# Spacing of the weight and activation buffers in SBUF: 8,192 to 8,288 bytes and 4,096 to 4,128 bytes

## The chip, the core and the metric

The kernel runs on one core of a Trainium2 chip. The metric is the device time of one execution in microseconds (us), median of three runs. TensorE multiplies (a weight load and a matmul are two instructions), VectorE (DVE), ScalarE (ACT) and GpSimd (POOL) do the elementwise work, and SyncE (SP) issues the loads from HBM into SBUF, the on-chip memory of 128 partitions. All byte addresses below are addresses within one partition.

## The reference

A two-layer decoder trunk on 256 tokens and 1,024 channels, all in float32. Each layer has a half-step SwiGLU block, a mixer (a gated linear recurrence in layer 0, causal pooling in layer 1), a second SwiGLU block, and a gated per-layer input:

```
for i in range(DEPTH):                                   # DEPTH = 2, D = 1024, D_FF = 2816, D_RNN = 1280
    h = h + 0.5 * swiglu(rms_norm(h, ffn1_norm[i]), ffn1_w_gate[i], ffn1_w_up[i], ffn1_w_down[i])
    hn = rms_norm(h, mix_norm[i])
    m = rglru_mixer(hn, ...) if i % 2 == 0 else pool_mixer(hn, ...)
    h = h + m
    h = h + 0.5 * swiglu(rms_norm(h, ffn2_norm[i]), ffn2_w_gate[i], ffn2_w_up[i], ffn2_w_down[i])
    gate = sigmoid(rms_norm(h, ple_norm[i]) @ ple_w_gate[i])
    h = h + gate * (p[i] @ ple_w_proj[i])
return rms_norm(h, final_norm)
```

## The kernel before

The activations lie transposed, channels on the partitions and the 256 tokens along the free axis. The weights come as units of 128 x 1,024 float32 (512 KB) in the order in which they are used. A unit is loaded into one of five buffers `raw` (`load`), and `split` makes of it two float32r halves, `hl[:, 0]` = the rounded value (ACT, line 272) and `hl[:, 1]` = the rest (DVE, line 273), in one of six buffers `hl`. The normalised input of a projection is split in the same way by `put` (ACT line 320, DVE line 321) into one of seven buffers `x`: high and low half, two column blocks of 256 tokens each. One product of a weight block with an activation block is then three matmuls in `mm3`: high x high, high x low, low x high. All of them are issued by the helper line 294. In each, a 128 x 128 block of `hl` is the stationary operand, 512 contiguous bytes a partition, loaded by a LDWEIGHTS of its own, and 256 columns of `x` (in the gate, up, recurrence and PLE projections), of `hid` (the down projection of the SwiGLU blocks), of `yr` and `ytp` (the recurrence's output projection) or of another `hl` unit (`pp`, the per-layer input) are the moving operand, 1,024 contiguous bytes. In `v` of the pooling mixer the sides are exchanged. Two kinds of matmul differ: `ri`, the gates of the recurrence, has plain float32 operands (`raw` and `xc`) and takes two passes, and `po`, the pooling operator, moves 144, 128 or 16 columns of an `hl` unit against a stationary `vhl`.

The order of the weights is written out in `stream_order`; loads run seven units ahead of use and splits four. The tile framework places a pool's buffers one behind the other, each rounded up to a multiple of 32 bytes. The kernel pads its narrow tiles to a multiple of 128 bytes itself:

```
LINE = 32
...
def lines(n):
    return -(-n // LINE) * LINE
```

In the program as it is built before the change, the six `hl` start at byte 40,064 + 8,192 i, the seven `x` at 101,504 + 4,096 j, and `hid`, `yr` and `ytp` behind them; each of these is 128 modulo 512, as the five `raw` are. A block of `hl` starts at a multiple of 512 bytes in its buffer and a block of a moving tile at a multiple of 1,024, so the distance from the stationary to the moving operand of these matmuls is 0 modulo 512. Two tiles lie elsewhere: the four `vhl` at 256 modulo 512, and the extra `raw` buffers of the recurrence's gates at 384.

Of the kernel before, what the change touches and what calls it, by code (L numbers as in the profile page):

```python
# [10 lines left out]
F32R = mybir.dt.float32r  # L11
# [4 lines left out]
P = 128  # L16
D = 1024
S = 256
# [10 lines left out]
U = 1024  # L29
# [92 lines left out]
def width(key):  # L122
    if key[0] == "lru_gates":
        return min(8, len(GATE_BLOCKS[key[1]]) - 8 * key[2]) * P
    if key[0] == "ple_in":
        return 2 * S
    if key[0] == "pool_op":
        return 4 * (POOL_COLS[key[1]][1] - POOL_COLS[key[1]][0])
    return U
# [81 lines left out]
def trunk(ctx: ExitStack, tc: tile.TileContext, xT, vec, w, out):  # L211
# [4 lines left out]
    hlp = ctx.enter_context(tc.tile_pool(name="hl", bufs=6))  # L216
    hp = ctx.enter_context(tc.tile_pool(name="h", bufs=6))
    xp = ctx.enter_context(tc.tile_pool(name="x", bufs=7))
# [27 lines left out]
    def vcol(name, i):  # L246
        c = VCOL[name] + i
        return vt[:, c:c + 1]
# [15 lines left out]
    def split(n, parts=1):  # L264
        if n not in raws:
            return
        raw = raws.pop(n)
        hl = hlp.tile([P, 2, U], F32R, tag="hl", name=f"hl{n}")
        step = width(ORDER[n]) // parts
        for i in range(parts):  # L270
            c = slice(i * step, (i + 1) * step)
            nc.scalar.activation(hl[:, 0, c], raw[:, c], AF.Copy)  # L272
            nc.vector.tensor_tensor(hl[:, 1, c], raw[:, c], hl[:, 0, c].bitcast(F32), op=ALU.subtract)  # L273
        units[ORDER[n]] = hl

    def unit(*key):
        n = state["used"]
        assert ORDER[n] == key, (ORDER[n], key)
        for what, do, ahead in (("loaded", load, LOADS_AHEAD), ("split", split, SPLITS_AHEAD)):
            while state[what] < min(n + ahead + 1, len(ORDER)):  # L280
                do(state[what])
                state[what] += 1
        state["used"] = n + 1
        return units.pop(key)
# [22 lines left out]
    class Norm:  # L307
# [6 lines left out]
            self.late = None  # L314

        def put(self, j, h, square=True):
            xt = xp.tile([P, 2, 2, S], F32R, tag="x", name=f"x{self.sid}_{j}")
            for c in range(2):
                g = vcol(self.name, 2 * j + c)
                nc.scalar.activation(xt[:, 0, c], h[:, c], AF.Copy, scale=g)  # L320
                nc.vector.scalar_tensor_tensor(  # L321
                    xt[:, 1, c], h[:, c], g, xt[:, 0, c].bitcast(F32), op0=ALU.mult, op1=ALU.subtract)
            self.x[j] = xt
            if square:
                self.square(j, h)
# [505 lines left out]
    load_x(0)  # L831
    load(0, 2)
    split(0, 4)
    load_x(1)
    load(1, 2)
    split(1, 4)
    load(2)
    load(3)
# [39 lines left out]
```

## Time and profile before

| | before |
|---|---|
| median of three runs | 982.45 us (982.06 to 984.19) |
| the profiled execution, its own time | 983.27 us |
| span from its first to its last instruction | 981.5 us |
| TensorE matmul / weight load busy | 967.3 us / 960.1 us |
| DVE / ACT / POOL busy | 652.4 us / 491.5 us / 54.8 us |
| mean granted TensorE clock | 0.996 |

The profiled execution's own time is 1.8 us longer than its span and 0.8 us above the median of the three runs. Matmuls overlap in the pipeline, so the busy share of TensorE says little; the time from one start to the next is what counts. A row that merges n instructions of a kind gives their first start and, in the chain of work, the time that n of them took.

### The profile page before, as it was taken

What the parts mean: (1) busy time and instruction counts of PE and PEld (TensorE: products, weight loads), DVE (VectorE), ACT (ScalarE), POOL (GpSimd) and SP (SyncE); (2) the same over time, 40 slices, a digit from 0 to 9 for tenths busy, and PEclk for the clock granted to TensorE, in tenths of its full rate; (3) what the DMA queues carried; (4) which work ended last, traced back from release to release, by engine and by line L of the source; (5) the groups of instructions that cost most, each with busy time, mean ns of one, the idle gap of its engine ahead of it and who ended that gap; (6) DMA issues with size and microseconds to landing.
All of it is one profiled execution on the core that took longest, in us unless ns stands there. A gap on an engine that the chain in (4) does not pass through costs nothing.

```text
span 981.5 us, 18712 instructions
## 1 busy us (share of the span) xinstructions
PE 967.3 (99%) x7888; PEld 960.1 (98%) x7888; DVE 652.4 (66%) x853; ACT 491.5 (50%) x634; POOL 54.8 (6%) x48
## 2 busy tenths in 40 slices
PE   9999999999999999999999999999989999999997
PEld 9999999999999999999998999999989999999996
DVE  6956555597887655655579756555578755555585
ACT  7544444468785444543456444444448544434443
POOL 1000000023201000000021000000011000000020
PEclk9999999999999999999999999999999999999999
DMA  8866556554435655565535655565524765655511
GB/s 294 281 210 190 179 179 189 167 178 172 151 114 168 204 192 172 193 197 189 175 126 173 215 178 188 173 193 172 183 90 146 242 192 171 195 190 174 192 44 44
DMA packets 49188, 173.63 MB, mean 177 GB/s; under 512 B 5584, under 2 KB 6224, under 8 KB 49104
## 3 DMA queue, kind: packets, MB, share of 16 engines
q1 hardware_dynamic: 48960, 172.29, 54.1%
q8 instruction: 61, 1.00, 0.4%
q14 instruction: 23, 0.19, 0.1%
q10 hardware_dynamic: 144, 0.15, 0.1%
HBM read 171.37 MB, written 1.05 MB: 176 GB/s over the span
## 4 chain that ended last, share of the span: by engine, by line
PE 72%; issue 20%; DVE 6%; ACT 1%; DMA 1%; POOL 0%; SPq 0%; DVEq 0%; ACTq 0%; POOLq 0%
PE up0ffn L294 13%; PE gate0ffn L294 13%; PE acc0ffn L294 12%; PE up1ffn L294 6%; PE gate1ffn L294 6%; PE acc1ffn L294 6%; PE accl L294 3%; PE gb L294 2%; PE ri L294 2%; DVE x L321 2%; PE x L294 2%; DVE hl L273 2%; PE pp L294 1%; PE xb L294 1%; PE ple L294 1%
## 5 line engine op out<-in xcount | busy, mean ns | idle before, releaser
L273 DVE TENSOR_TENSOR hl<-raw,hl 128x1024 fp32r<-128x1024 f32 (+1 forms) x326 | 385.6, 1200 | 242.0 <-ACT hl L272 242.0
L272 ACT ACTIVATE hl<-raw 128x1024 fp32r<-128x1024 f32 (+1 forms) x326 | 331.9, 1035 | 413.2 <-issue 103.0
L294 PE MATMUL gate1ffn<-x,hl 128*128 128x256 f32 x1056 | 132.6, 284 | 2.2 <-DVE x L321 2.1
L294 PE MATMUL gate0ffn<-x,hl 128*128 128x256 f32 x1056 | 132.5, 284 | 0.3 <-ACT x L320 0.2
L294 PEld LDWEIGHTS gate1ffn<-x,hl 128*128 128x128 f32 x1056 | 129.0, 192 | 3.2 <-DVE x L321 3.0
L294 PE MATMUL up1ffn<-x,hl 128*128 128x256 f32 x1056 | 132.0, 283 | 0.0
L294 PE MATMUL up0ffn<-x,hl 128*128 128x256 f32 x1056 | 131.3, 283 | 0.0
L294 PE MATMUL acc0ffn<-hid,hl 128*128 128x256 f32 x1056 | 130.3, 283 | 0.0
L294 PEld LDWEIGHTS gate0ffn<-x,hl 128*128 128x128 f32 x1056 | 129.1, 192 | 1.0 <-ACT x L320 0.4
L294 PE MATMUL acc1ffn<-hid,hl 128*128 128x256 f32 x1056 | 130.0, 283 | 0.0
L294 PEld LDWEIGHTS up1ffn<-x,hl 128*128 128x128 f32 x1056 | 128.9, 192 | 0.0
L294 PEld LDWEIGHTS up0ffn<-x,hl 128*128 128x128 f32 x1056 | 128.6, 192 | 0.0
L294 PEld LDWEIGHTS acc0ffn<-hid,hl 128*128 128x128 f32 x1056 | 128.2, 192 | 0.2
L294 PEld LDWEIGHTS acc1ffn<-hid,hl 128*128 128x128 f32 x1056 | 128.2, 192 | 0.0
L334 POOL TENSOR_TENSOR sacc<-sq,sq 128x512 f32<-128x512 f32 x9 | 14.3, 1588 | 844.8 <-ACT sq L329 844.8
L321 DVE SCALAR_TENSOR_TENSOR x<-h,vt,x 128x256 fp32r<-128x256 f32 x64 | 48.7, 800 | 7.1 <-ACT x L320 7.1
L294 PE MATMUL ple<-x,hl 128*128 128x256 f32 x384 | 47.5, 284 | 0.0
L294 PEld LDWEIGHTS ple<-x,hl 128*128 128x128 f32 x384 | 46.6, 192 | 0.0
L466 ACT ACTIVATE hid<-gs 128x512 fp32r<-128x512 f32 x44 | 27.9, 634 | 16.4 <-DVE gs L464 16.3
L320 ACT ACTIVATE x<-h,vt 128x256 fp32r<-128x256 f32 x64 | 28.4, 496 | 6.0 <-DMA vt<-vec 2.5
L464 DVE TENSOR_TENSOR gs<-th,gs 128x512 f32<-128x512 f32 x44 | 30.4, 692 | 1.4
L467 DVE TENSOR_TENSOR hid<-gs,hid 128x512 fp32r<-128x512 f32 x44 | 30.1, 685 | 0.0
(132 smaller groups left out, 692.8 us busy)
## 6 DMA issues: line engine op xcount, KB each, us to landing
raw<-w SPq DMA_DIRECT2D x320, 512.0 KB, 4.2
raw<-w SPq DMA_DIRECT2D x7, 256.0 KB, 4.5
h<-xT SPq DMA_DIRECT2D x4, 256.0 KB, 6.5
out<-hg SPq DMA_DIRECT2D x3, 256.0 KB, 2.8
raw<-w SPq DMA_DIRECT2D x1, 288.0 KB, 2.6
raw<-w SPq DMA_DIRECT2D x2, 128.0 KB, 4.4
out<-hg SPq DMA_DIRECT2D x2, 128.0 KB, 2.0
vt<-vec ACTq DMA_DIRECT2D x1, 148.0 KB, 4.4
```

The costliest lines, as they stand in the source:

```text
L272: nc.scalar.activation(hl[:, 0, c], raw[:, c], AF.Copy)
L273: nc.vector.tensor_tensor(hl[:, 1, c], raw[:, c], hl[:, 0, c].bitcast(F32), op=ALU.subtract)
L294: nc.tensor.matmul(o, lhsT, rhs, start=self.first, stop=self.left == 0, skip_group_check=True)
L320: nc.scalar.activation(xt[:, 0, c], h[:, c], AF.Copy, scale=g)
L321: nc.vector.scalar_tensor_tensor(xt[:, 1, c], h[:, c], g, xt[:, 0, c].bitcast(F32), op0=ALU.mult, op1=ALU.subtract)
L334: nc.gpsimd.tensor_tensor(acc, self.acc, sq, op=ALU.add)
L464: nc.vector.tensor_tensor(gs, th, gs, op=ALU.mult)
L466: nc.scalar.activation(hid[:, 0], gs, AF.Copy)
L467: nc.vector.tensor_tensor(hid[:, 1], gs, hid[:, 0].bitcast(F32), op=ALU.subtract)
```

## The change

The tile of a weight unit is allocated 24 floats (96 bytes) longer, that of an activation 8 floats (32 bytes) longer, and the same view as before is cut out of the front. No instruction is added or removed, and each engine's instructions stand in the same order as before.

```diff
-        hl = hlp.tile([P, 2, U], F32R, tag="hl", name=f"hl{n}")
+        hl = hlp.tile([P, 2 * U + 24], F32R, tag="hl", name=f"hl{n}")[:, :2 * U].rearrange("p (v u) -> p v u", v=2)
...
-            xt = xp.tile([P, 2, 2, S], F32R, tag="x", name=f"x{self.sid}_{j}")
+            xt = xp.tile([P, 4 * S + 8], F32R, tag="x", name=f"x{self.sid}_{j}")[:, :4 * S].rearrange("p (v c s) -> p v c s", v=2, c=2)
```

In the program as it is built with the change, the start addresses modulo 512 are:

| tiles | before | changed |
|---|---|---|
| six `hl` | 128, all | 128, 224, 320, 416, 0, 96 |
| seven `x` | 128, all | 192, 224, 256, 288, 320, 352, 384 |
| `hid`, `yr`, `ytp`, `xc`, `gs`, `th`, `sq`, `hg` and the rest behind `x` | 128 | 416 |
| residual `h` (between `hl` and `x`) | 128 | 192 |
| `vhl` of the pooling mixer | 256 | 32 |
| `raw` of the recurrence's gates | 384 | 160 |
| `raw`, vectors | 128 | 128 |

## Rows read from the trace of the kernel before

**Rows 1.** The page's first lines: span, and busy time of each engine.

```profile
span 981.5 us, 18712 instructions
PE 967.3 (99%) x7888; PEld 960.1 (98%) x7888; DVE 652.4 (66%) x853; ACT 491.5 (50%) x634; POOL 54.8 (6%) x48
```

**Rows 2.** The page's slices: TensorE's granted clock in tenths, 40 equal slices.

```profile
PEclk9999999999999999999999999999999999999999
```

**Rows 3.** Groups of matmuls by shape: stationary and moving names, count, busy us, mean ns.

```profile
L294 PE MATMUL gate1ffn<-x,hl 128*128 128x256 f32 x1056 | 132.6, 284 | 2.2 <-DVE x L321 2.1
...
L294 PE MATMUL acc0ffn<-hid,hl 128*128 128x256 f32 x1056 | 130.3, 283 | 0.0
...
L294 PE MATMUL ple<-x,hl 128*128 128x256 f32 x384 | 47.5, 284 | 0.0
L294 PE MATMUL accl<-yr,hl 128*128 128x256 f32 x160 | 28.9, 283 | 0.0
L294 PE MATMUL gb<-x,hl 128*128 128x256 f32 x192 | 23.5, 284 | 0.0
...
L294 PE MATMUL accl<-ytp,hl 128*128 128x256 f32 x80 | 22.6, 283 | 0.0
L294 PE MATMUL x<-x,hl 128*128 128x256 f32 x144 | 17.9, 284 | 0.0
L294 PE MATMUL pp<-hl,hl 128*128 128x256 f32 x96 | 13.4, 303 | 0.0
```

**Rows 4.** The chain that ended last: start us, us, engine, tile, count.

```profile
43.95 5.76 PE up0ffn L294 x48
...
187.96 11.52 PE acc0ffn L294 x96
...
223.90 11.23 PE ri L294 x52
...
280.90 28.79 PE accl L294 x240
```

**Rows 5.** Timeline of the weight loads around the pooling operator: start us, us, count.

```profile
744.35 4.55 PEld L294 LDWEIGHTS po<-hl,vhl 128*128 128x128 f32 x40
748.83 0.66 PEld L294 LDWEIGHTS pp<-hl,hl 128*128 128x128 f32 x5
```

**Rows 6.** The tile po: count, shortest, median and longest duration ns, forms.

```profile
L294 PE MATMUL po<-hl,vhl x40: 216/276/308, 744.5 to 748.8; 128*128 128x144 f32 x16, 128*128 128x128 f32 x16, 128*128 128x16 f32 x8
```

**Rows 7.** Lines 680, 630 and 632: count, shortest, median and longest duration ns.

```profile
L680 ACT ACTIVATE r<-r,zero,sp_sp x10: 585/588/601, 237.7 to 275.3; 128x256 f32<-128x256 f32 x10
...
L630 ACT ACTIVATE xc<-xbs,vt x10: 582/587/601, 218.7 to 249.1; 128x256 f32<-128x256 f32 x10
...
L632 DVE SCALAR_TENSOR_TENSOR xc<-xbs,vt,xc x30: 456/479/486, 219.4 to 253.1; 128x256 f32<-128x256 f32 x30
```

**Rows 8.** Who waited for whom, TensorE: us in total, times, longest us.

```profile
PE v L294 <- DVE x L321: 2.6, 4, 0.8
PE gate1ffn L294 <- DVE x L321: 2.1, 4, 0.7
PE spread L378 <- DVE dg L377: 1.3, 1, 1.3
```

**Rows 9.** The page's costliest groups, splits of weights: busy us, mean ns.

```profile
L273 DVE TENSOR_TENSOR hl<-raw,hl 128x1024 fp32r<-128x1024 f32 (+1 forms) x326 | 385.6, 1200 | 242.0 <-ACT hl L272 242.0
L272 ACT ACTIVATE hl<-raw 128x1024 fp32r<-128x1024 f32 (+1 forms) x326 | 331.9, 1035 | 413.2 <-issue 103.0
```

**Rows 10.** The page's DMA issues: count, KB each, us from issue to landing.

```profile
raw<-w SPq DMA_DIRECT2D x320, 512.0 KB, 4.2
...
h<-xT SPq DMA_DIRECT2D x4, 256.0 KB, 6.5
out<-hg SPq DMA_DIRECT2D x3, 256.0 KB, 2.8
```

## The prediction, made before the changed kernel was run

> **What bounds the kernel now.** I read the page's first lines, then the groups of matmuls, then the chain of waits, then single stretches of the timeline. [...] The longest waits of TensorE for another engine come to 2.6, 2.1 and 1.3 us in all [rows 8]. So TensorE's own pace sets the end, and the question is what sets that pace.
>
> The chain gives it without the overlap of the pipeline: 48 matmuls of an up projection in 5.76 us, 96 of a down projection in 11.52, 240 of the recurrence's output in 28.79 [rows 4]. Each is 120 ns from start to start, to a tenth, whichever tiles feed it. The groups shown with 256 columns of a float32r operand count 6 x 1,056 (gate, up and down in both layers; two of the six rows stand there) + 384 + 160 + 192 + 80 + 144 + 96 = 7,392 matmuls [rows 3]; three small groups are left out. 7,392 x 0.120 = 887.0 us, 90% of the span. Nothing else in the kernel has such a lever: one ns on this pace is 7.4 us of the end.
>
> What is in the 120 ns? Two other rows bound its two halves. The gates of the recurrence, plain float32 in two passes, take 11.23 us for 52 [rows 4], 216 ns for one; the load of the weights hides under them, so the moving side alone needs at most 108 ns a pass, if a pass streams half of that time. And where the pooling operator moves few columns, the loads set the pace: the first of 40 starts at 744.35, the load after the last at 748.83 [rows 5], 4.48 us / 40 = 112 ns. So 120 is 8 ns more than the longer of the two halves, at a place where both operands are read at once and where their distance is 0 modulo 512. Those 8 ns are all that a better placing could win: 7,392 x 8 = 59.1 us.
>
> **The change part by part.** *Instructions and order:* none is added, removed or moved, so no wait is added and no queue is passed. Cost 0.
>
> *The distance of the two operands.* After the change the down projections read `hid` at 416 against `hl` at six different starts, the gate and up projections 42 pairs. No row of before shows 256 columns at another distance than 0, so the cost is bounded. The nearest row is the pooling operator: its `vhl` lies at 256, its moving blocks at 128 plus 64 bytes per group of channels in the first half of the tokens (576 bytes a group), so the four groups are 384, 448, 0 and 64 apart. Its matmuls move 144, 128 or 16 columns [rows 6], and its 40 loads come at 112 ns over the whole stretch [rows 5]. If distance 0 cost the third group's ten loads the 8 ns in question, or the other distances cost the other thirty as much, the mean would be 2 or 6 ns above that of the rest; but all forty come at 112 ns, without a break in the row, 8 ns below the pace of the long matmuls on either side. Distance 0 in one group of the four doesn't bring the 120 back. I choose 0 for the distance, since this row is the nearest. The bounds stay: a gain of up to 8 ns a matmul, and a loss for which there is no row with 256 columns.
>
> [...]
>
> *The starts themselves.* Before, all these operands start on the 128-byte grid that the kernel keeps for its narrow tiles. After it, four of six `hl` (224, 320, 416, 96), five of seven `x` and all of `hid`, `yr` and `ytp` start off it, at other multiples of 32. On TensorE the rows that touch this are again the pooling operator's: its second and fourth group move blocks that start 64 bytes off the grid, and the mean of its loads doesn't show it. But no row shows a *weight* block off the grid, so a loss there is open from 0 upward. On ACT two rows compare directly: line 680 reads 256 elements from the grid with a scale and a bias column, line 630 does the same from 12 bytes off it, and they take 588 and 587 ns [rows 7]. On DVE line 632 reads the same tile from 8, 4 and 0 bytes past the grid, and its 30 instructions lie between 456 and 486 ns with a median of 479 [rows 7]. An engine that needed a further access for a crossed line would show it in these. I take 0 for ACT and DVE. Cover, if it were not: the splits take 1,200 ns on DVE and 1,035 on ACT for 326 units [rows 9], four units ahead of use; 10 ns more on each of DVE's 326 would be 3.3 us out of the 329 us in which DVE isn't busy (981.5 - 652.4, [rows 1]). Uncovered are the `x` tiles at the layer boundaries: some 64 instructions of line 321, of which TensorE waited for eight; 10 ns on each of the eight is 0.1 us.
>
> *DMA.* The main `raw` buffers don't move, so the 320 loads of 512 KB [rows 10] write where they did. `h`, the extra `raw` of the gates and the output tiles move. Their loads run ahead of use, except that of `h` at the start (6.5 us to landing) and the stores at the end (2.8 us) [rows 10]; a hundredth on these is 0.1 us. I take 0.
>
> **The sum.** 0 + 0 + 0 on the profiled execution's 983.27 us (span 981.5 and 1.8 around it). That execution stands 0.8 us above the median of 982.45 us, so I forecast the median, **982.5 us**.
>
> **The rivals.** *Slower: a weight block off the grid costs its load something.* The load is the longer half (112 against 108), so what it loses, the pace loses. For: no row excludes it, and every one of the 7,392 matmuls has an operand off the grid except where one of the two aligned `hl` meets an aligned `x`. Against: ACT, DVE and the moving side of `po` show nothing. Price: the smallest step that the trace can show is 1 ns; 7,392 x 1 = 7.4 us, so **989.9 us**. It decides (0.2% is 2.0 us, about what a measurement of this kernel can tell from no change) from 2.0 / 7,392 = 0.27 ns a matmul. [...]
>
> [...]
>
> *Faster: the 8 ns are two reads at distance 0 in each other's way.* For: 120 is above both halves, and the two reads begin together in each matmul. Against: the third group of `po` has distance 0 too and its loads aren't longer. The whole price, 59.1 us, would give 923.3; but the pooling rows leave room for a part at most, and I choose a quarter, 2 ns a matmul: 14.8 us, so **967.7 us**. It decides from the same 0.27 ns.
>
> [...]
>
> *The change doesn't do what it says.* If the allocator rounded tiles up to 512 bytes, nothing would move. The starts in the changed program exclude that, so it gets no chance of its own. That the new starts don't touch the pace is the forecast itself.
>
> **How the numbers follow.** No change within 0.2%: 0.54, from the 112 ns over four distances and the equal ACT and DVE rows. Slower: 0.25, since no row shows a weight block off the grid, and a quarter of a ns decides. Faster: 0.21, since 8 ns are unexplained. The range reaches to the slower rival's 1 ns (989.9) and, on the other side, to nearly the faster rival's 2 ns (967.7): 970 to 990. Left out is somewhat over a half of the faster case and a quarter of the slower one, some 0.17 together. The likeliest case alone lies between 980.5 and 984.4.
>
> **What would show it.** In the changed trace's chain, 48 up or down matmuls in 5.76 us and 240 of the recurrence's output in 28.79 confirm the forecast. A pace that differs by `hl` buffer, with a period of six units, 5.9 us here and 5.76 there, would speak for a cost of starts or distances; a uniform change of the pace would speak for distances only if the down projections, with one `hid` start against six `hl`, differ from the gates. ACT's and DVE's splits should stay at 1,035 and 1,200 ns. The forecast is wrong if the pace moves by more than a quarter of a ns, either way; it would then be the step that carries over the pooling operator's short matmuls to 256 columns.

## The result, and the profile after

The changed kernel takes 970.42 us (969.80 to 971.52, three runs) against 982.45: a ratio of 0.9875, 95% interval 0.9852 to 0.9898. It is 12.0 us faster. The forecast was no change; the time lies in the range, at its lower end, near where the *faster* rival stood (967.7). One execution of one experiment kernel further down (the first under "Setting the pace from distance 0") took 2,393.67 us where its other three took 969.85 to 970.90; it is left out of that kernel's numbers, and as it is the one that was traced, no pace is read from that kernel.

The page's first lines of the changed kernel, and three of its costliest groups:

```profile
span 968.6 us, 18712 instructions
PE 952.8 (98%) x7888; PEld 944.8 (98%) x7888; DVE 652.1 (67%) x853; ACT 491.5 (51%) x634; POOL 55.5 (6%) x48
PEclk9999999999999999999999999999998999999999
L273 DVE TENSOR_TENSOR hl<-raw,hl 128x1024 fp32r<-128x1024 f32 (+1 forms) x326 | 385.6, 1201 | 234.6 <-ACT hl L272 234.6
L272 ACT ACTIVATE hl<-raw 128x1024 fp32r<-128x1024 f32 (+1 forms) x326 | 332.2, 1036 | 398.9 <-issue 97.2
L294 PEld LDWEIGHTS up1ffn<-x,hl 128*128 128x128 f32 x1056 | 127.3, 188 | 0.0
```

DVE and ACT are as busy as before [rows 1, 9], to a ns per split, so the off-grid starts cost them nothing, as forecast. What shrank is TensorE: matmuls from 967.3 to 952.8 us, loads from 960.1 to 944.8. A weight load is recorded with 188 ns, where the kernel before has 192:

```profile
L294 PEld LDWEIGHTS up1ffn<-x,hl 128*128 128x128 f32 x1056 | 128.9, 192 | 0.0
```

The clock doesn't explain it: the mean granted clock was 0.996 before and 0.994 in this execution.

The timeline of TensorE's matmuls in layer 0 of the changed kernel (start us, us, tile, count) shows the pace itself:

```profile
65.97 5.84 PE L294 MATMUL acc0ffn<-hid,hl 128*128 128x256 f32 x48
71.64 5.83 PE L294 MATMUL gate0ffn<-x,hl 128*128 128x256 f32 x48
77.31 5.85 PE L294 MATMUL up0ffn<-x,hl 128*128 128x256 f32 x48
83.00 5.84 PE L294 MATMUL acc0ffn<-hid,hl 128*128 128x256 f32 x48
```

Read the first column: from one down projection to the next 144 matmuls take 83.00 - 65.97 = 17.03 us, 118.3 ns each, where it was 120.0 [rows 4]. Over all 7,584 float32r matmuls with 256 columns the intervals from start to start add up to 922.5 us before and 909.8 after (a sum of the trace's starts): 12.7 us less, and the span is 12.9 shorter. So the gain lies between the starts of these matmuls. The pace alone would give more: some 7,490 of the intervals are between 110 and 130 ns long, and their mean fell by 1.98 ns, which is 14.8 us. The others, most of them longer, took 23.2 us before and 25.9 after. That is no more than two kernels at the same 120 ns further down differ in (19.0 us in the one at distance 0 off the grid, 25.2 in the one at 256), so no cause is read from it.

The prediction's sign for distances, down projections that differ from the gates, doesn't show in these rows: their starts are 5.67 to 5.69 us apart, whatever the tile. Each row of 48 mixes two `hl` buffers and up to four `x` buffers, so it mixes distances too.

The prediction's nearest row, the pooling operator, did not change. The weight loads there:

```profile
735.18 4.55 PEld L294 LDWEIGHTS po<-hl,vhl 128*128 128x128 f32 x40
739.65 0.66 PEld L294 LDWEIGHTS pp<-hl,hl 128*128 128x128 f32 x5
```

40 loads in 4.47 us, 112 ns, as in [rows 5], although `hl` and `vhl` lie elsewhere now. At no distance that they have in either kernel do the loads beside these short matmuls show what the long ones show.

Sorted by distance, the trace of the changed kernel says more. The table takes the intervals of 110 to 130 ns between two successive 256-column float32r matmuls, by the distance of the block that is being loaded (for the next matmul) from the moving operand of the matmul that is running, modulo 256 bytes, stationary minus moving start. *Settled* is the mean from the seventh interval on of stretches that stay at one distance (modulo 512) for ten or more.

| distance modulo 256 | intervals | mean ns | settled ns |
|---|---|---|---|
| 0 | 1,356 | 119.0 | 119.6 to 119.7 |
| 32 | 732 | 118.2 | 118.1 |
| 64 | 908 | 115.7 | 113.9 and 116.0 |
| 96 | 1,295 | 118.0 | 117.9 to 118.2 |
| 128 | 638 | 118.5 | 118.5 |
| 160 | 1,031 | 119.6 | 119.9 to 120.2 |
| 192 | 916 | 117.0 | 117.6 to 117.8 |
| 224 | 608 | 117.2 | 116.5 to 116.9 |

Where two numbers stand, they are the two distances modulo 512, which hardly differ, but for 64. The starts themselves matter little beside it: at distance 32 the settled means lie between 118.0 and 118.5 ns over six different pairs of starts modulo 256, and at no distance but 64 do they spread by more than 1.5 ns. This gave the theory that the experiments test: **the pace of a long matmul depends on the distance between the stationary block being loaded and the moving operand being read, with a period of 256 bytes, and 0 is among the worst**. (A matmul's own two operands are at the same distance in all but the matmuls at a change of buffer, so the runs don't tell the two readings apart.) Rivals: the starts themselves (off the 128-byte grid), the spreading as such, or the shift of the other buffers.

### The profile page after: what moved, and what is told of

Same layout as the page of the kernel before. It is cut to its first block, busy times and chain, and to the rows that moved or that the text cites. A ratio compares the mean times of both kernels' runs of the same rounds, so it can differ in the third digit from the quotient of the medians.

```text
span 968.6 us, 18712 instructions
## 1 busy us (share of the span) xinstructions
PE 952.8 (98%) x7888; PEld 944.8 (98%) x7888; DVE 652.1 (67%) x853; ACT 491.5 (51%) x634; POOL 55.5 (6%) x48
## 4 chain that ended last, share of the span: by engine, by line
PE 65%; issue 20%; DVE 9%; ACT 3%; DMA 1%; POOL 0%; SPq 0%; DVEq 0%; ACTq 0%; POOLq 0%
PE up0ffn L294 13%; PE gate0ffn L294 13%; PE acc0ffn L294 12%; PE up1ffn L294 6%; PE gate1ffn L294 6%; PE acc1ffn L294 6%; DVE hl L273 3%; DVE x L321 2%; PE x L294 2%; PE accl L294 1%; PE pp L294 1%; PE ri L294 1%; ACT hl L272 1%; PE ple L294 1%; DMA h<-xT 1%
## 5 line engine op out<-in xcount | busy, mean ns | idle before, releaser
L273 DVE TENSOR_TENSOR hl<-raw,hl 128x1024 fp32r<-128x1024 f32 (+1 forms) x326 | 385.6, 1201 | 234.6 <-ACT hl L272 234.6
L272 ACT ACTIVATE hl<-raw 128x1024 fp32r<-128x1024 f32 (+1 forms) x326 | 332.2, 1036 | 398.9 <-issue 97.2
L294 PE MATMUL gate0ffn<-x,hl 128*128 128x256 f32 x1056 | 130.5, 281 | 0.7 <-ACT hl L272 0.5
L294 PEld LDWEIGHTS gate1ffn<-x,hl 128*128 128x128 f32 x1056 | 127.0, 188 | 3.6 <-DVE x L321 3.0
L294 PEld LDWEIGHTS gate0ffn<-x,hl 128*128 128x128 f32 x1056 | 126.9, 189 | 1.5 <-ACT hl L272 0.7
L294 PE MATMUL acc0ffn<-hid,hl 128*128 128x256 f32 x1056 | 128.2, 281 | 0.0
L294 PE MATMUL acc1ffn<-hid,hl 128*128 128x256 f32 x1056 | 126.6, 279 | 0.0
L294 PEld LDWEIGHTS acc0ffn<-hid,hl 128*128 128x128 f32 x1056 | 126.0, 189 | 0.2 <-ACT hid L466 0.2
L294 PEld LDWEIGHTS acc1ffn<-hid,hl 128*128 128x128 f32 x1056 | 124.7, 189 | 0.0
```

The lines of the kernel that those rows point to most:

```text
L294: nc.tensor.matmul(o, lhsT, rhs, start=self.first, stop=self.left == 0, skip_group_check=True)
```

## The experiments

All kernels compute the whole reference; only addresses differ. Where several runs share a chip, the kernel before took 982.9 to 983.1 us there.

**Distance 64 everywhere.** The kernel before, with unused bytes between the `h` and the `x` pool:

```diff
+    ctx.enter_context(tc.tile_pool(name="gap", bufs=1)).tile([P, 112], F32, name="gap")
     xp = ctx.enter_context(tc.tile_pool(name="x", bufs=7))
```

> Kernel before with 448 unused bytes between the residual and the activation buffers: weight buffers 8,192 apart at 128 modulo 512 as before, all moving tiles at 64, so stationary minus moving start is 64 modulo 512 in nearly every matmul. Distance theory (period 256): the changed kernel's stretches at 64 modulo 256 ran at 113 to 114 ns from start to start, so 48 matmuls take 5.44 us and the time is 982.45 - 7,584 x 6.6 ns = 932 us. Theory that only spreading over many distances helps, or that weight blocks off the 128-byte grid are what is quicker: no spread here and no weight block off the grid, so 982 us (5.76 us for 48).

959.27 us (956.50 to 963.33), ratio 0.9768 (0.9731 to 0.9805). One constant distance, no spread and all weight blocks on the grid beat the changed kernel; so neither the spreading nor weight blocks off the grid are needed for the gain. (The moving tiles are off it here, at 64; the next kernel and the last two, whose moving tiles are on it, answer that.) But 932 was missed by 27 us. The timeline of the matmuls shows why:

```profile
373.85 5.82 PE L295 MATMUL up0ffn<-x,hl 128*128 128x256 f32 x48
379.50 5.82 PE L295 MATMUL acc0ffn<-hid,hl 128*128 128x256 f32 x48
385.16 5.92 PE L295 MATMUL pp<-hl,hl 128*128 128x256 f32 x48
390.92 5.63 PE L295 MATMUL gate0ffn<-x,hl 128*128 128x256 f32 x48
...
401.82 5.60 PE L295 MATMUL acc0ffn<-hid,hl 128*128 128x256 f32 x48
407.26 5.60 PE L295 MATMUL gate0ffn<-x,hl 128*128 128x256 f32 x48
412.70 5.60 PE L295 MATMUL up0ffn<-x,hl 128*128 128x256 f32 x48
```

Up to 385 the starts are 5.65 us apart, 117.7 ns a matmul; behind `pp` (two `hl` units, distance 0, 5.76 us or 120 ns) they are 5.44 apart, 113.3 ns. The same distance has two steady paces, and each holds for hundreds of matmuls until something interrupts. The changed kernel's trace had both already: of its 29 stretches of ten or more at 64, 14 settled at 113.2 to 113.4 ns and 15 at 117.6 to 117.8. The means of 113.9 and 116.0 in the table hid that, and the expectation took the fast one for all. In this execution 1,614 of 7,513 intervals were at 115 ns or less.

**Distance 0 off the grid.** The same spare tile, of 32 bytes, ahead of the weight buffers, so that all operands start at 160 modulo 512.

```diff
+    ctx.enter_context(tc.tile_pool(name="gap", bufs=1)).tile([P, 8], F32, name="gap")
     hlp = ctx.enter_context(tc.tile_pool(name="hl", bufs=6))
```

> Kernel before with 32 unused bytes ahead of the weight buffers: all weight and moving tiles start at 160 modulo 512, 32 bytes off the 128-byte grid, at distance 0 as before. Distance theory: 120 ns, 982.5 us, within 0.2%. Theory of the starts (off the grid is quicker): the gain of the changed kernel, 970 us or less. If a weight block off the grid cost something: above 984.5 us.

982.25 us, ratio 1.0002 (0.9988 to 1.0015). Starts 32 bytes off the grid neither help nor hurt; the prediction's *slower* rival falls with the theory of the starts.

```profile
95.61 5.92 PE L295 MATMUL up0ffn<-x,hl 128*128 128x256 f32 x48
101.37 5.92 PE L295 MATMUL acc0ffn<-hid,hl 128*128 128x256 f32 x48
107.13 5.92 PE L295 MATMUL gate0ffn<-x,hl 128*128 128x256 f32 x48
```

The starts are 5.76 us apart as in the kernel before.

**Distance 256.** The spare tile in front of `x` has 256 bytes (64 floats).

> Kernel before with 256 unused bytes between residual and activation buffers: distance 256 (stationary 128, moving 384 modulo 512) everywhere. Distance theory with a period of 256: it settles at 120 ns as distance 0 does, 48 in 5.76 us, 982 us within 0.3%. With a period of 512, where the farthest is the best: well below 970 us. Theory of conflicts with other engines' buffers, which the shift of everything behind moves: a gain of its own, of any size.

983.43 us, ratio 1.0006 (0.9993 to 1.0019).

```profile
95.32 5.92 PE L295 MATMUL up0ffn<-x,hl 128*128 128x256 f32 x48
101.08 5.92 PE L295 MATMUL acc0ffn<-hid,hl 128*128 128x256 f32 x48
```

5.76 us again: 256 acts as 0. And moving all buffers behind `x` by 256 bytes does nothing by itself.

**Distance 192.** The spare tile has 320 bytes (80 floats).

> Kernel before with 320 unused bytes between residual and activation buffers: distance 192 (stationary 128, moving 448 modulo 512). Distance theory, from the changed kernel's stretches at 192 and 448, which settle at 117.7 ns: 982.45 - 7,584 x 2.3 ns = 965 us, 48 matmuls in 5.65 us. If it is only a matter of being apart, the same as the kernel at distance 64. Starts theory: no weight block moves, 982 us.

968.79 us, ratio 0.9863 (0.9839 to 0.9886). The pace is as forecast from the changed kernel's stretches, and nearly all of it has one value (216 of 7,491 intervals are at 115 ns or less):

```profile
94.40 5.82 PE L295 MATMUL up0ffn<-x,hl 128*128 128x256 f32 x48
100.06 5.82 PE L295 MATMUL acc0ffn<-hid,hl 128*128 128x256 f32 x48
105.71 5.81 PE L295 MATMUL gate0ffn<-x,hl 128*128 128x256 f32 x48
```

5.65 to 5.66 us for 48, 117.7 ns. The mean interval, 117.67 ns, is what was expected; the end misses its 965 by 4 us, and the intervals outside 110 to 130 ns, which no expectation counted, take 26.0 us here against 23.2 before. 64 and 192 differ, so "apart" isn't enough either.

**The two halves of the change, alone.** First the weight spacing only (the `x` tile as before):

```diff
-            xt = xp.tile([P, 4 * S + 8], F32R, tag="x", name=f"x{self.sid}_{j}")[:, :4 * S].rearrange("p (v c s) -> p v c s", v=2, c=2)
+            xt = xp.tile([P, 2, 2, S], F32R, tag="x", name=f"x{self.sid}_{j}")
```

> Only the weight buffers are 96 bytes farther apart; all moving tiles start at 192 modulo 512. Distance theory (period 256): the six buffers stand at 192, 32, 128, 224, 64 and 160 modulo 256 from them, and by the changed kernel's stretches settle at 117.7, 118.1, 118.5, 116.6, 114 and 118.5 ns, 117.2 in the mean: 982.9 - 7,584 x 2.7 ns = 962 us, 959 to 968 with what a change of distance costs. If both spacings are needed, or only that of the activations acts: 975 to 983 us.

968.68 us (965.51 to 969.99), ratio 0.9858 (0.9833 to 0.9882); the mean interval is 117.6 ns. Then the activation spacing only (the `hl` tile as before):

```diff
-        hl = hlp.tile([P, 2 * U + 24], F32R, tag="hl", name=f"hl{n}")[:, :2 * U].rearrange("p (v u) -> p v u", v=2)
+        hl = hlp.tile([P, 2, U], F32R, tag="hl", name=f"hl{n}")
```

> Only the activation buffers are 32 bytes farther apart; weight blocks all at 128 modulo 512, on the grid. Distance theory: the down projections at distance 32 modulo 256 (118.1 ns), the others at 0, 224, 192, 160, 128, 96 and 64 (117.6 in the mean): 982.9 - 7,584 x 2.1 ns = 967 us, 963 to 971. Theory that the weight buffers' spread is what acts: 982 us.

970.96 us (969.12 to 972.86), ratio 0.9886 (0.9865 to 0.9907). Either half alone gives about what both give: each takes most matmuls away from distance 0, and there isn't a second gain to add. The first missed its point (962) by 7 us, the second (967) by 4; the first had put 160 down with 118.5 ns, where the table above has 119.9 to 120.2 and this kernel's mean is 119.9. Its pace, 117.6 instead of 117.2, is 3 us of the 7; the intervals outside 110 to 130 ns take 28.1 us against 23.2 before, which is most of the rest.

**Distances 80 and 48.** The weight view starts 16 bytes into its tile, which is 256 bytes longer so that all six buffers agree modulo 256; the spare tile in front of `x` has 448 and 480 bytes.

```diff
-        hl = hlp.tile([P, 2, U], F32R, tag="hl", name=f"hl{n}")
+        hl = hlp.tile([P, 2 * U + 64], F32R, tag="hl", name=f"hl{n}")[:, 4:2 * U + 4].rearrange("p (v u) -> p v u", v=2)
```

> As the kernel at distance 64, with the weight blocks 16 bytes farther: distance 80 modulo 256 everywhere. The kernel at 64 ran in two paces, 113.3 and 117.7 ns. If 64 stands at the edge of a good region that reaches toward 96: mostly 113 to 114 ns, 932 to 945 us. If the good region lies below 64: 118 ns as at 96 in the changed kernel, 968 us. If it is narrower than 16 bytes: 118 ns too.

> As the kernel at distance 64, with a distance of 48 modulo 256 everywhere. If 64 stands at the edge of a good region that reaches toward 32: mostly 113 to 114 ns, 932 to 945 us. If the good region lies above 64, or is narrower than 16 bytes: 118 ns as at 32 in the changed kernel, 968 us.

973.05 us (ratio 0.9912, 0.9891 to 0.9933) and 970.42 us (0.9889, 0.9853 to 0.9924); mean intervals 118.7 and 117.9 ns. Neither has the fast pace:

```profile
95.01 5.86 PE L295 MATMUL up0ffn<-x,hl 128*128 128x256 f32 x48
100.70 5.86 PE L295 MATMUL acc0ffn<-hid,hl 128*128 128x256 f32 x48
...
94.46 5.82 PE L295 MATMUL up0ffn<-x,hl 128*128 128x256 f32 x48
100.11 5.82 PE L295 MATMUL acc0ffn<-hid,hl 128*128 128x256 f32 x48
```

The starts are 5.69 us apart at 80 (the first two lines) and 5.65 at 48. So 16 bytes to either side the fast pace of 64 is gone. The weight blocks of these two kernels also start 16 bytes off a multiple of 32, which those of no other kernel do; no run parts that from the distance.

**Setting the pace from distance 0.** Since one pace of the two held at 64 depending on what stood before, a unit out of six gets another distance (all `hl` tiles and all moving tiles at 128 modulo 256, the weight view 4 `at` bytes further on):

```diff
+        odd = ORDER[n][2] == "gate" and ORDER[n][4] == 0 if ORDER[n][0] in ("ffn1", "ffn2") else n % 6 == 0
+        at = 0 if odd else 16
-        hl = hlp.tile([P, 2, U], F32R, tag="hl", name=f"hl{n}")
+        hl = hlp.tile([P, 2 * U + 64], F32R, tag="hl", name=f"hl{n}")[:, at:at + 2 * U].rearrange("p (v u) -> p v u", v=2)
```

> Distance 64 everywhere, but 0 in one unit out of six (the first half of each gate block, 24 matmuls in a row): 1,350 matmuls at 0, 6,214 at 64. Theory: at 64 there are two steady paces, 113.3 and 117.7 ns, and which one holds depends on how the loads and matmuls stood to each other when the stretch began; in the three spread kernels 33 of 33 stretches at 64 after five or more matmuls at 0 ran at 113.6 to 114.3. Then 982.9 - (7,584 x 120 - 1,350 x 120 - 6,234 x 113.6) ns = 943 us, up to 950 with the breaks between. Rival, each 64-stretch falls by chance to one or the other: 960 us or more. Rival, the time depends on the mean distance alone: between 959 and 983 us.

970.21 us (969.85 to 970.90), ratio 0.9870 (0.9853 to 0.9886). The theory of what sets the pace fell: worse than distance 64 alone by 11 us. With the odd unit in every second gate block only (`ORDER[n][3] % 2 == 0` added to the condition):

> As the kernel with one unit of six at distance 0, but only in every second gate block: 870 matmuls at 0, 6,694 at 64. If the faster pace, once set, holds: 982.9 - (7,584 x 120 - 870 x 120 - 6,714 x 113.6) ns = 940 us. If it is lost at the breaks between stages and blocks: no better than its companion, 945 to 955 us.

968.73 us, ratio 0.9855 (0.9837 to 0.9873): neither 940 nor 945 to 955.

```profile
93.04 5.82 PE L296 MATMUL up0ffn<-x,hl 128*128 128x256 f32 x48
98.69 5.82 PE L296 MATMUL acc0ffn<-hid,hl 128*128 128x256 f32 x48
104.34 5.87 PE L296 MATMUL gate0ffn<-x,hl 128*128 128x256 f32 x48
110.05 5.82 PE L296 MATMUL up0ffn<-x,hl 128*128 128x256 f32 x48
```

48 matmuls take 5.65 us behind the odd unit: the slow pace. By the starts, all 23 stretches at 64 behind 24 matmuls at 0 ran at 117.7 or 117.8 ns, up to the next interruption at least (two of them went on at 113.3 after one). In the stretches on which the expectation rested, nearly all of them in the kernel with the activation spacing alone, the moving operand had moved (there the weight block stayed); here the weight block moves. So if what comes before sets the pace, it isn't by its distance alone.

**The control: distance 192 in the odd unit** (`at = 48`).

> As the kernel with one unit of six at distance 0, but with that unit at distance 192. In the changed kernel all six stretches at 64 behind one at 192 ran at 117.7 ns. If the matmuls at distance 0 are what sets the faster pace: 117.7 ns nearly everywhere, 982.9 - 7,584 x 2.25 ns = 966 us. If any interruption of distance 64 serves: about 945 us, as the kernel with 0.

947.13 us (945.39 to 948.09), ratio 0.9632 (0.9616 to 0.9647). The time is near the 945 that was put down for "any interruption serves", but the kernel with 0 took 970, so that isn't the reason. What was expected of 192 failed the other way round: here 39 of 39 stretches at 64 behind 24 matmuls at 192 ran at 113.3 or 113.4 ns, up to the next interruption at least. (The premise doesn't show in the changed kernel's trace: sorted as in the table, no stretch at 64 stands directly behind one at 192 there.)

```profile
92.10 5.60 PE L296 MATMUL up0ffn<-x,hl 128*128 128x256 f32 x48
97.54 5.60 PE L296 MATMUL acc0ffn<-hid,hl 128*128 128x256 f32 x48
102.98 5.60 PE L296 MATMUL gate0ffn<-x,hl 128*128 128x256 f32 x48
```

48 in 5.44 us throughout, the gate block with its half at 192 included: the mean over the 1,291 intervals at 192 is 114.5 ns here, where it was 117.7 in the kernel at 192 alone; so 192 has the fast pace too. 6,031 of 7,503 intervals are at 115 ns or less.

**More entries from 192.** The last kernel puts the first half of each gate, up, recurrence and PLE block at 192:

```diff
-        odd = ORDER[n][2] == "gate" and ORDER[n][4] == 0 if ORDER[n][0] in ("ffn1", "ffn2") else n % 6 == 0
+        odd = ORDER[n][0] != "lru_out" and ORDER[n][2:3] != ("down",) and ORDER[n][-1] == 0
```

> As the kernel with one unit of six at distance 192, but the first half of every gate, up, recurrence and PLE block lies there, so that a stretch at 64 begins behind one at 192 every 48 matmuls instead of every 144. In that kernel 39 of 39 stretches at 64 behind 24 matmuls at 192 ran at 113.3 ns, and 117.7 was left only between a break and the next such stretch (some 1,450 of 7,493 intervals at 116 ns or more). If the entry from 192 is what sets the pace: most of these fall to 113 to 114 ns, 1,000 x 4.4 ns = 4 us less, 941 to 945 us. If every change of distance costs: 947 us or more.

945.90 us (943.06 to 946.23), ratio 0.9609 (0.9589 to 0.9629). All 74 stretches at 64 behind 24 at 192 ran at 113.3 or 113.4 ns, and 6,448 of 7,486 intervals are at 115 ns or less; the end is just outside what was expected, and its interval overlaps that of the kernel before it. Both are some 23 to 25 us below the changed kernel. Behind another number of matmuls (five or more) the entry decides less: from 0 four of ten stretches at 64 took the fast pace in the kernel with the odd unit in every second gate block, from 192 thirteen of 23 in the last two kernels.

## Why the prediction was wrong

- *TensorE's pace is the lever, 120 ns, one ns worth 7.4 us:* right. The change moved that pace by 1.98 ns in the mean (119.96 to 117.98 over the intervals of 110 to 130 ns) and the end by 12.0 us: 14.8 us of pace, less some 2 in the longer intervals of the traced executions.
- *No cost in DVE, ACT, DMA or order:* right; the splits stayed at 1,201 and 1,036 ns, the loads of 512 KB still land after 4.2 us, and the kernel with all starts off the grid but distance 0 takes the same time as before.
- *The moving side needs at most 108 ns:* misread, without weight in the sum. The program has 26 matmuls in the stretch of [rows 4] that shows 52 records of `ri`, two for each, so 216 ns is one pass and not a matmul of two; halving it had no ground. What the runs show is that load and stream together go down to 113.3 ns, 1.3 above the 112 of the load beside short matmuls.
- *The distance costs and gives nothing:* this step failed. It rested on the pooling operator's 40 loads at 112 ns over four distances. That row is right and was the same after the change (of the third group's ten loads six, and not ten, stand at distance 0, and they come at 112 ns too), but its matmuls move at most 144 columns. It gives the pace of the loads beside those short matmuls in these two kernels, 112 ns (in the kernel at distance 64 the same 40 matmuls take 4.73 us from start to start, 118 ns each, against 4.42 us before); it says nothing of a load beside 256 columns. In place of the 0 the runs showed 1.98 ns a matmul. The step that carried it over is the one the prediction had named as the place where it would fail. The kernels at 0 and 256 (120.0 ns), 192 (117.7) and 64 (113.3 or 117.7) differ in one unused tile alone and show the dependence; those at 80 (118.7) and 48 (117.9) fit it.
- *The faster rival:* right that distance 0 costs something, and nearly right in size. Its quarter of the 8 ns, 2 ns a matmul, was a choice, not a reading; that 1.98 was measured is luck. The settled paces that it averages lie between 113.3 and 120.2 ns, and distance 160 is as slow as 0, so it isn't only equal starts that cost. 14.8 us were worked out and 12.0 came.
- *"Against" the rival stood that the group of `po` at distance 0 isn't slower.* True, and of no weight, for the same reason.
- *The slower rival:* excluded by the kernel off the grid, to about 0.15%, for weight blocks 32 bytes off it.

With the instructions the same, moving the activation buffers by 256 bytes leaves the mean interval at 119.97 ns, and moving them by 448 brings it to 116.9: where the two operands lie counts for the pace. How the two reads meet inside the memory isn't shown by any run here.

What decides between the two paces at distance 64 stays open. An entry from 192 gave the fast one (113 of 113 stretches behind 24 matmuls), an entry from 0 by a shift of the weight block the slow one (23 of 23 behind 24), an entry from 0 by a shift of the moving tile, in the kernel with the activation spacing alone, the fast one (25 of 25 stretches of ten or more matmuls, settled at 113.2 to 113.4 ns). Behind fewer or more matmuls than 24 both paces follow, so these counts are no rule. That the two operands' relative timing is what is carried over was only argued, and the starts don't show it: in the kernel at 64 nearly every load starts 2 to 5 ns behind the running matmul, at either pace.

## What to carry to other kernels

When long matmuls run at a constant pace that is slower than that of the weight loads beside short ones, compare the addresses of the stationary and the moving operand before blaming the instruction: a spare tile of a few hundred bytes between two pools is the whole experiment. Here that alone was worth 24 us of 983 (distance 64); with the first half of most blocks at 192 it was 37. Don't average over distances where one can be chosen; and test a chosen distance over whole stages, since one distance may have two paces (113.3 and 117.7 ns at 64 here). A row that bounds a cost must have the size of the thing bounded: 144 columns didn't speak for 256.

## What the hardware showed that wasn't expected

- The distance acts modulo 256 bytes: 0 and 256 give 119.97 ns in the mean.
- It is sharp: 113.3 ns at 64, and at 48 and 80 the fast pace is gone (weight blocks 16 bytes off a multiple of 32 in both).
- The same program has two steady paces at one distance, 4.4 ns apart: 113.3 and 117.7 ns at 64. At 192 the kernel at 192 alone has 117.7 ns in the mean, and the one with 192 in the odd unit of six, the rest at 64, 114.5 over its intervals at 192. The runs at distance 64 spread from 956.5 to 963.3 us, those at 192 from 968.4 to 969.2. That the two paces are the reason isn't shown: one execution of each was traced, and the kernel at 48, which lacks the fast pace, spread from 968.1 to 976.1.
- After nearly each interruption in the kernel before, a few matmuls ran below 120 ns before the pace settled (in 29 of 30 stretches of eight or more, an interval of 113 to 118 ns among the first eight). The load durations from 187 to 192 ns within one tile were its trace (over the intervals of 110 to 130 ns in that kernel, those that end at a matmul whose load took 187, 188 or 189 ns have means of 117.4, 118.2 and 119.1 ns, those of a load of 192 ns 120.0), and weren't read as such:

```profile
L294 PEld LDWEIGHTS up1ffn<-x,hl x1056: 187/192/192, 531.4 to 929.7; 128*128 128x128 f32 x176
```
